# Four of eight token tiles turned by VectorE block transposes and transfers in SBUF, after the w_out product

## The chip, the cores and the metric

The kernel runs on one core of one Trainium2 chip. The metric is device time in microseconds of one execution, the median of several runs. A core has five instruction queues: TensorE (PE; its weight loads are listed as PEld), VectorE (DVE), ScalarE (ACT), GpSimd (POOL) and SyncE (SP), which here issues nearly all DMAs.

## The reference

One layer of a hybrid decoder on 1024 tokens, with 16 meta tokens ahead of them, model width 1024:

```python
z = h @ w_in + b_in                                   # q, k, v, convolution input, gates
y_attn = swa_sink_attention(q, k, v, ...) @ w_attn_proj
y_conv = silu(layer_norm(causal_dwconv(c, ...), ...)) @ w_conv_proj
mixed = sigmoid(g_attn) * y_attn + sigmoid(g_conv) * y_conv
h = layer_norm(DEEPNORM_ALPHA * h + mixed @ w_out, ln1_g, ln1_b)
up = causal_dwconv(h @ ffn_w_up, ffn_dw, ffn_dw_b)
u, g = jnp.split(up, 2, axis=-1)
f = (jax.nn.gelu(g, approximate=False) * u) @ ffn_w_down
return layer_norm(DEEPNORM_ALPHA * h + f, ln2_g, ln2_b)
```

The change sits at the line with w_out: the product, the residual, the LayerNorm, and the turn of its result into the layout that the next product, `h @ ffn_w_up`, needs.

## The kernel before

All matrix products are in float32 accuracy by splitting each operand into a high and a low part (float32r) and adding three products: high by high, high by low, low by high. ScalarE casts the high part, VectorE or GpSimd subtracts it to get the low part. `product` issues such a sum on TensorE.

The w_out product works on eight tiles of 128 tokens, with tokens on the partitions and the 1024 channels along the row. The order is 3, 7, 2, then the two last meta tokens (-1), 6, 0, 4, 1, 5. For each tile `out_rows` does two halves of 512 columns of 24 matmuls each into a PSUM bank `ps_w`; VectorE adds the residual row from `h0d` in DRAM (L1339), takes statistics (L1340), and after the second half normalizes the row (L1361). Newton's step for the reciprocal root goes through ScalarE (L268) and three small VectorE operations. The normalized row `r` lies in one of two 1024-column buffers of `RT` (part of `OB`), is stored to `h1d` in DRAM for the residual of the feed-forward part, and the buffer then takes the row load of the tile after next.

The next product needs the channels on the partitions. `turn` transposes a tile on TensorE in eight 128x128 pieces into two PSUM banks `ps_h` (L1375), and ScalarE copies them into `FA` with the LayerNorm gain and bias as scale and shift (L1385). The turn of a tile is queued on TensorE inside the tile behind it, after a half of its product, and the other half is queued after the turn. The last tile, 5, is turned inside the up projection.

The up projection is done by Strassen's scheme on 2x2 blocks, in two passes: first on `sub` 1 (the second 256 tokens of each half of the tokens: tiles 2, 3, 6, 7), then on `sub` 0 (tiles 0, 1, 4, 5). VectorE forms sums of blocks (`bsub`, L1285), and ScalarE and VectorE split them (`bsplit`, L1276 and L1281); weights are split by `wsplit` (L1405, L1406) and combined by VectorE (L1423). These steps are done between the tiles, listed in `work`, and from tile 0 on VectorE's order is written out: every operation that goes through `line` is queued behind the one before it. All other order on an engine is the scheduler's, which works with ranks (`RK_TURN` comes before `RK_SUMS`); `after` adds an order without a wait of its own. SyncE issues loads and stores in one order for all, and a DMA that has to wait holds those behind it.

Of the kernel before, what the change touches and what calls it, by code (L numbers as in the profile page):

```python
# [25 lines left out]
AF = mybir.ActivationFunctionType  # L26
# [3 lines left out]
P = 128  # L30
D = 1024
KC = D // P
# [29 lines left out]
SUB = [(0, 258), (258, HW)]  # L62


RK_TURN, RK_SPLIT, RK_EVAC, RK_START, RK_QKV, RK_RESID, RK_ATT = 450, 500, 600, 1000, 10000, 20000, 30000
# [59 lines left out]
def tile_hybrid_layer(  # L125
# [3 lines left out]
    nc = tc.nc  # L129
# [5 lines left out]
    def load(o, i):  # L135
        return nc.sync.dma_start(out=o, in_=i)
# [5 lines left out]
    def f32(ap):  # L142
        return ap.bitcast(F)

    def after(ins, first):

        tc.add_manual_dep(ins.ins, first.ins.name, mybir.DependencyInfo(
            mybir.DependencyClass.NoSync, mybir.DependencyReason.SCHED_ONLY), reason="order of work")

    @contextmanager  # L150
    def rank(p):

        saved = tc.cur_priority
        tc.cur_priority = p
        yield
        tc.cur_priority = saved
# [10 lines left out]
    RHC = arena.tile([P, 8384], R, name="RHC")  # L167
    RHO = arena.tile([P, 8384], R, name="RHO")
    OB = arena.tile([P, 4 * U], F, name="OB")
# [6 lines left out]
    h0d = dpool.tile([U, D], F, name="h0d")  # L176
    h1d = dpool.tile([S, D], F, name="h1d")
# [39 lines left out]
    cols = const.tile([P, N_COLS], F, name="cols")  # L217
# [13 lines left out]
    g1col = lambda k: colA[:, 58 + k:59 + k]  # L231
    b1col = lambda k: colA[:, 66 + k:67 + k]
# [420 lines left out]
    for k in range(8):  # L653
        scaled(2, k)
        parts(2, k, hi_act=(1, 3, 5, 7))
        if k in (3, 4, 5, 6):
# [26 lines left out]
    bias, bias0 = (bias_t[:, a:b].rearrange("p (u h c) -> p u h c", u=2, h=NH // 2)  # L683
                   for a, b in ((0, NH * KW), (NH * KW, N_BIAS)))
# [60 lines left out]
    src = ps[:16, :P].rearrange("p (g d) -> p g d", d=HD)  # L745
    nc.scalar.copy(VA[:16, 0, :, 0], src)
    nc.vector.tensor_tensor(VA[:16, 0, :, 1], src, f32(VA[:16, 0, :, 0]), OP.subtract)
    for q4 in range(2):
# [4 lines left out]
        src = ps[:, :].rearrange("p (n g d) -> p n g d", g=2, d=HD)  # L753
# [16 lines left out]
    def load_q(g, i):  # L770
        m = 0 if i else 16
        t = ap.tile([P, 8 * P + 16], R, name="qt", tag="qt", bufs=3)[:, 16 - m:]
        for h in range(2):
            load(f32(t[h * HD:(h + 1) * HD]), dram(qd, g * HD * 8 * U + q_at(i) - m, [[8 * U, HD], [1, 8 * P + m]]))
        if m:
            pairs0.append(t[:, :16].rearrange("p (l r q) -> p l r q", l=2, r=4))
        return t[:, m:].rearrange("p (u l h x) -> p l u h x", l=2, u=2, h=2)
# [7 lines left out]
    ahead = chunks_done[first_chunk + 2 * KC + 7]  # L785
# [6 lines left out]
    for h in range(NH):  # L792
        g, r = divmod(h, 4)
        o = ps[:2, h * 16:(h + 1) * 16]
# [34 lines left out]
    for g in range(NKV):  # L829
# [3 lines left out]
        src = ps[:16].rearrange("p (r q) -> p r q", r=4)[:, :, 0:2]  # L833
# [3 lines left out]
    for g in range(NKV):  # L837
        o = po[:, g * 8:g * 8 + 8]
# [21 lines left out]
    for i in range(NB):  # L860
        for g in range(NKV):
            q = load_q(g, i) if i else q0[g]
# [6 lines left out]
            for u in range(2):  # L869
# [3 lines left out]
                for h in range(2):  # L873
                    o = ps[:, h * KW:h * KW + w]
# [8 lines left out]
                if not i:  # L883
                    f = first[u]
                    src = ps[:, :2 * KW].rearrange("p (h c) -> p h c", h=2)
# [9 lines left out]
            for h in range(2):  # L895
                for u in range(2):
                    j = h * 2 + u
# [68 lines left out]
    OC = late.tile([P, 8320], R, name="OC")  # L966
# [124 lines left out]
    RT = OB[:, 0:2048]  # L1091
# [128 lines left out]
    def h1_at(sub, i):  # L1220
        return 2048 * sub + i * (SUB[sub][1] - SUB[sub][0])

    def h1F(sub, h, k):
        o = h1_at(sub, h * KC + k)
        return FA[:, o:h1_at(sub, h * KC + k + 1)]
# [28 lines left out]
    def line(ins):  # L1254

        if lined:
            after(ins, lined[-1])
        lined.append(ins)
        return ins
# [51 lines left out]

    WO_ORDER = (4, 5, 0, 1, 2, 3, 6, 7)
    edge = const.tile([P, KC, 2], F, name="edge")
    r_next = [1]

    def out_rows(i, between=(), work=()):


        n, u = (P, 2 + i * P) if i >= 0 else (2, 0)
        if n == P:  # L1320
            o = r_next[0] % 2 * 1024
            r_next[0] += 1
            whole = RT[:, o:o + 1024]
            load(whole, h0d[u:u + n, :])
        else:
            whole = OB[:, 3072:4096]
        r = whole[:n]
        order = WO_ORDER if i != 5 else (0, 1, 2, 3, 6, 7, 4, 5)
        turned = None
        st = small.tile([P, 2, 6], F, name="st")  # L1330
        pin = line if i in (0, 4, 1, 5) else lambda ins: ins
        for half in range(2):
            hs = slice(half * 512, half * 512 + 512)
            ps = pat.tile([P, 512], F, name="ps_w", tag="mm", bufs=3)
            if n == P:
                last = product(ps, [(mixed(i, k, 0), mixed(i, k, 1), wo[k][0][:, hs], wo[k][1][:, hs])
                                    for k in order], turned)
                with rank(RK_TURN):
                    pin(nc.vector.tensor_tensor(r[:, hs], ps, r[:, hs], OP.add))  # L1339
                    pin(nc.vector.bn_stats(st[:, half], r[:, hs]))  # L1340
                turned = None
                if between[half:] and between[half]:
                    turned = turn(*between[half], behind=[last])
                if half == 0:
                    for f, *x in work:
                        f(*x)
                continue

            for j in range(4):
                nc.tensor.matmul(ps[:2], sel[:, j // 2 * 2:j // 2 * 2 + 2], two_parts[j // 2][j % 2][:, hs],  # L1350
                                 start=j == 0, stop=j == 3)
            nc.scalar.copy(r[:, hs], ps[:2])
        if n < P:
            q = FA[:2, 0:1024]
            load(q, h0d[0:2, :])
            nc.vector.tensor_tensor(r, r, q, OP.add)
        with rank(RK_TURN):
            (mu, rs), = ln_stats([(r, n)], half_stats=st if n == P else None)
            for a in (512, 0) if i == 5 else (None,):
                x = r if a is None else r[:, a:a + 512]  # L1360
                ins = pin(nc.vector.tensor_scalar(x, x, mu, rs, OP.subtract, OP.mult))  # L1361
        if n == P:
            load(h1d[u - 2:u - 2 + P, :], r)
        else:
            load(ed, r)
            for t in range(2):
                load(edge[:, :, t], dram(ed, t * D, [[1, P], [P, KC]]))
        return whole, n, ins

    def turn(i, r, n, ins, banks=None, behind=None, upper=False):  # L1370
        with rank(RK_TURN):
            for j, k0 in enumerate((4, 0) if upper else (0, 4)):
                ps = banks[j] if banks else pat.tile([P, 512], F, name="ps_h", tag="s", bufs=2)
                for k in range(4):
                    ins = nc.tensor.transpose(ps[:, k * P:(k + 1) * P], r[:, (k0 + k) * P:(k0 + k + 1) * P], ident)  # L1375
                    if behind:
                        after(ins, behind[-1])
                        behind.append(ins)
                for k in range(k0, k0 + 4):
                    src = ps[:, (k - k0) * P:(k - k0 + 1) * P]  # L1380
                    h, jj = divmod(i, 4)
                    sub = 0 if jj < 2 else 1
                    a = 2 + jj * P - SUB[sub][0]
                    dst = h1F(sub, h, k)[:, a:a + P]
                    nc.scalar.activation(dst, src, AF.Identity, bias=b1col(k), scale=g1col(k))  # L1385
        return behind[-1] if behind else None


    RING = [RHO[:, i * 1024:(i + 1) * 1024] for i in range(4)]
    RING += [None] * 4  # L1390
# [81 lines left out]
    ahead = []  # L1472
# [4 lines left out]
    for i in (3, 7, 2, -1, 6, 0, 4, 1, 5):  # L1477
        if i == -1:
            out_rows(i)
            continue  # L1480
        rows = out_rows(i, ahead, work.get(i, ()))
        ahead = [None, (i, *rows)] if i == 3 else [(i, *rows)]
        if i == 3:
            two_rows(7, rows[2])
        if i == 7:
            for a, (hi, lo) in zip(two_sum, two_parts):
                after(split(a, hi, lo, True), rows[2])
            two_stack.close()
            W2.append(wo_stack.enter_context(tc.tile_pool(name="w2", bufs=1, side="right", reuse_waits="tile")).tile(
                [P, 2048], R, name="W2"))  # L1490
        if i == 0:
            form_t2(1)
        if i == 4:
            split_of(1, BT4)
            split_of(1, BT1)
            edges()
        if i == 1:
            split_of(1, BT3)
            split_of(0, B21, EARLY)
            form_t3(0, EARLY)  # L1500
            form_t4(0, EARLY)
# [64 lines left out]
    for c in range(FC):  # L1566
# [8 lines left out]
        for subs in passes:  # L1575
            last = subs == passes[-1]
            w_next = iter(range(7))
            a, b = SUB[subs[0]][0], SUB[subs[-1]][1]
            i = max(a, 2)
# [37 lines left out]
            ins = tt(c11[:, a:b], at(Z), u13[:, a:b], OP.add)  # L1617
# [23 lines left out]
            ins = tt(c22[:, i:b], c22[:, i:b], u13[:, i:b], OP.add)  # L1641
# [127 lines left out]
    rows, stats = {}, {}  # L1769
# [159 lines left out]
```

## Time and profile before

| | |
|---|---|
| median of 3 runs | 1234.69 us (1234.56 to 1234.72) |
| profiled execution | 1234.65 us |
| its span in the profile | 1232.9 us, 21777 instructions |
| TensorE, VectorE, ScalarE, GpSimd busy | 99%, 88%, 47%, 1% |
| DMA | 210.62 MB, mean 171 GB/s |
| product of w_out to start of the up projection | about 490 to 588 us from the start of the span |

A row of the timeline has the start in us from the start of the span, the duration in us, the engine, the line of the kernel, the operation, what it writes and reads, the shape and the count of merged instructions; in brackets stands how long the engine was idle before it and what ended that. SPq is the DMA issue on SyncE. Tiles of the work (3, 7, 2, ...) are not named in the rows; they follow from the order.

### The profile page before, as it was taken

The page shows a single profiled execution, that of the slowest core. Times are in us where ns is not written, and L with a number is a line of the kernel's source. Part 1 is how long each engine was busy: PE and PEld are TensorE (multiplying, and loading weights), DVE is VectorE, ACT ScalarE, POOL GpSimd, SP SyncE. Part 2 cuts the span into 40 slices and gives each one's busy share as a digit, 9 for nine tenths or more (in the row PEclk, how much of TensorE's full clock was granted, in tenths as well). Part 3 has the DMA queues.
Part 4 walks back from the last instruction along what each step waited for, and adds up shares of the span by engine and source line. Part 5 has one row for each costly group of instructions (what it writes and reads, how often), then busy time and mean ns, then how long its engine had stood idle before and what let it go on. Part 6 is the DMA issues. An engine that isn't in the chain of part 4 may idle for free.

```text
span 1232.9 us, 21777 instructions
## 1 busy us (share of the span) xinstructions
PE 1223.6 (99%) x8564; PEld 1141.3 (93%) x8564; DVE 1084.5 (88%) x1840; ACT 584.4 (47%) x1065; POOL 15.0 (1%) x19
## 2 busy tenths in 40 slices
PE   9999999999999999999999999999999999999997
PEld 8999999999999999888999999999999998888886
DVE  8899989999879798659899999998999986995697
ACT  7532346654265233435655545555455553544331
POOL 1000000000000010000000000000000000000000
PEclk9999999999999999999999999999999999999999
DMA  7284834412255544322255555554465568997722
GB/s 280 74 277 101 213 96 112 129 55 73 85 153 175 180 140 136 116 73 87 69 182 197 193 191 197 191 187 137 167 210 190 182 230 305 395 334 295 255 87 86
DMA packets 104726, 210.62 MB, mean 171 GB/s; under 512 B 28520, under 2 KB 42394, under 8 KB 104624
## 3 DMA queue, kind: packets, MB, share of 16 engines
q1 hardware_dynamic: 88624, 198.16, 48.6%
q10 hardware_dynamic: 16000, 11.07, 2.9%
q8 instruction: 67, 1.10, 0.4%
q14 instruction: 35, 0.29, 0.1%
HBM read 147.59 MB, written 60.38 MB: 169 GB/s over the span
## 4 chain that ended last, share of the span: by engine, by line
PE 98%; DVE 1%; ACT 0%; issue 0%; DMA 0%; POOL 0%; DVEq 0%; POOLq 0%
PE px L1596 14%; PE py L1596 9%; PE ps_x L1742 9%; PE ps_z L330 8%; PE ps_z L329 8%; PE ps_z L325 8%; PE ps_z L1742 8%; PE pw L1596 5%; PE pz L1596 5%; PE ps_p L325 2%; PE ps_p L329 2%; PE ps_p L330 2%; PE ps_w L329 2%; PE ps_w L330 2%; PE ps_w L325 2%; PE ps_z L565 2%
## 5 line engine op out<-in xcount | busy, mean ns | idle before, releaser
L715 DVE SCALAR_TENSOR_TENSOR FA<-cin,cols,FA 128x1026 f32<-128x1026 f32 x120 | 152.3, 1278 | 0.9
L330 PE MATMUL ps_z<-RHO,wlo 128*128 128x256 f32 (+2 forms) x324 | 103.6, 320 | 0.0
L329 PE MATMUL ps_z<-RHO,whi 128*128 128x256 f32 (+2 forms) x324 | 103.5, 319 | 0.0
L330 PE MATMUL ps_z<-RHC,wlo 128*128 128x256 f32 (+2 forms) x324 | 103.4, 319 | 0.0
L329 PE MATMUL ps_z<-RHC,whi 128*128 128x256 f32 (+2 forms) x324 | 103.4, 319 | 0.0
L325 PE MATMUL ps_z<-RHC,whi 128*128 128x256 f32 (+2 forms) x324 | 103.2, 319 | 0.0
L325 PE MATMUL ps_z<-RHO,whi 128*128 128x256 f32 (+2 forms) x324 | 103.2, 318 | 0.0
L294 ACT CAST whi<-wr 128x1024 fp32r<-128x1024 f32 x37 | 38.9, 1051 | 107.4 <-PE ps_z L329 85.1
L1405 ACT CAST RHO<-wr 128x512 fp32r<-128x512 f32 x92 | 55.3, 619 | 26.2 <-DMA wr<-in_w_up_dram 12.2
L1406 DVE TENSOR_TENSOR RHO<-wr,RHO 128x512 fp32r<-128x512 f32 x92 | 62.4, 690 | 5.2 <-ACT RHO L1405 4.9
L325 PEld LDWEIGHTS ps_z<-RHO,whi 128*128 128x128 f32 x324 | 60.9, 188 | 4.5
L329 PEld LDWEIGHTS ps_z<-RHO,whi 128*128 128x128 f32 x324 | 60.9, 188 | 4.2
L325 PEld LDWEIGHTS ps_z<-RHC,whi 128*128 128x128 f32 x324 | 60.9, 188 | 4.1
L329 PEld LDWEIGHTS ps_z<-RHC,whi 128*128 128x128 f32 x324 | 61.0, 188 | 4.1
L330 PEld LDWEIGHTS ps_z<-RHO,wlo 128*128 128x128 f32 x324 | 61.0, 188 | 4.0
L330 PEld LDWEIGHTS ps_z<-RHC,wlo 128*128 128x128 f32 x324 | 61.0, 188 | 3.9
L1423 DVE TENSOR_TENSOR wr<-wr 128x512 f32<-128x512 f32 x88 | 60.9, 692 | 0.2
L297 DVE TENSOR_TENSOR wlo<-wr,whi 128x1024 fp32r<-128x1024 f32 x35 | 42.7, 1221 | 12.0 <-ACT whi L294 11.6
L1608 ACT COPY FA<-px 128x514 f32<-128x514 f32 (+2 forms) x23 | 13.1, 569 | 71.1 <-PE px L1596 71.0
L1405 ACT CAST ws<-wr 128x512 fp32r<-128x512 f32 x60 | 36.1, 618 | 20.9 <-DVE wr L1423 11.8
L722 ACT ACTIVATE FA<-ps_z,cols 128x258 f32<-128x258 f32 (+2 forms) x48 | 26.1, 543 | 39.4 <-PE ps_z L330 39.0
L1406 DVE TENSOR_TENSOR ws<-wr,ws 128x512 fp32r<-128x512 f32 x60 | 40.6, 688 | 3.6 <-ACT ws L1405 3.5
(487 smaller groups left out, 3492.2 us busy)
## 6 DMA issues: line engine op xcount, KB each, us to landing
wr<-in_w_up_dram SPq DMA_DIRECT2D x44, 512.0 KB
wr<-in_w_z_dram SPq DMA_DIRECT2D x30, 512.0 KB
fd<-FA SPq DMA_DIRECT2D x44, 256.0 KB
OB<-in_w_down_dram SPq DMA_DIRECT2D x19, 512.0 KB
qt<-qd SPq DMA_DIRECT2D x28, 256.0 KB
td<-OB SPq DMA_DIRECT2D x12, 512.0 KB
sums<-fd SPq DMA_DIRECT2D x12, 512.0 KB
sd<-sums SPq DMA_DIRECT2D x12, 512.0 KB
```

Of the source, the lines that this page charges most:

```text
L294: ins = nc.scalar.copy(hi, raw)
L297: return (nc.vector if quick else nc.gpsimd).tensor_tensor(lo, raw, f32(hi), OP.subtract)
L325: ins = nc.tensor.matmul(ps, ah, bh, start=i == 0, stop=False)
L329: nc.tensor.matmul(ps, ah, bl, start=False, stop=False)
L330: last = nc.tensor.matmul(ps, al, bh, start=False, stop=i == n - 1)
L715: nc.vector.scalar_tensor_tensor(acc[c], cin[:, j:j + U], wc, acc[c], OP.mult, OP.add)
L722: nc.scalar.activation(t, ps, AF.Tanh, bias=bcol(14 + i), scale=0.5)
L1405: nc.scalar.copy(hi, src)
L1406: ins = nc.vector.tensor_tensor(lo, src, f32(hi), OP.subtract)
L1423: ins = nc.vector.tensor_tensor(*x)
L1596: ins = nc.tensor.matmul(o, x[:, ks], bmat(sub, q, hl, k), start=first and k + j == 0, stop=k == 3 and j == 2, skip_group_check=not first)
L1742: nc.tensor.matmul(bank[:, cs], l[:, ts], r[:, ws], start=first and a and x + k == 0, stop=z and x == len(ops) - 1 and k == 2, skip_group_ ...
```

## The change

Tiles 3, 7, 2 and 0 are no longer turned on TensorE. After the normalization VectorE does one `transpose` over 128x1024, which turns every 32x32 block in its place and sorts the blocks by the partition group they go to; 16 transfers in SBUF (32 partitions of 1 KB each) bring the blocks to their partitions, into a free stretch of `OC` or `RHC`; and eight ScalarE copies read them from there into `FA` with the same scale and shift as before. For tile 0 the transpose has a place in VectorE's written order, right after the normalization. Tiles 6, 4, 1 and 5 are turned as before.

The row loads, the stores of normalized rows and the transfers get one written order on SyncE (`in_turn`): the load of the tile after next comes after the tile's transfers, or, for tiles turned on TensorE, after the turn. Before, these were in the scheduler's order.

```diff
+    NROW = (3, 7, 2, 6, 0, 4, 1, 5)
+    NEXT_ROWS = dict(zip(NROW, NROW[2:]))
+    moves, fetched = [], {}
+
+    def in_turn(ins):
+        if moves:
+            after(ins, moves[-1])
+        moves.append(ins)
+
+    def fetch(i):
+        o = (NROW.index(i) + 1) % 2 * 1024
+        fetched[i] = RT[:, o:o + 1024]
+        in_turn(load(fetched[i], h0d[2 + i * P:2 + (i + 1) * P, :]))
...
         if n == P:
-            o = r_next[0] % 2 * 1024
-            r_next[0] += 1
-            whole = RT[:, o:o + 1024]
-            load(whole, h0d[u:u + n, :])
+            if i not in fetched:
+                fetch(i)
+            if not moves[1:]:
+                fetch(NROW[1])
+            whole = fetched[i]
...
                     turned = turn(*between[half], behind=[last])
+                    if between[half][0] in NEXT_ROWS:
+                        fetch(NEXT_ROWS[between[half][0]])
...
-            load(h1d[u - 2:u - 2 + P, :], r)
+            in_turn(load(h1d[u - 2:u - 2 + P, :], r))
...
+    TURN_AT = {3: (OC, 4144, 2048), 7: (OC, 5168, 2048), 2: (OC, 6192, 2048), 0: (RHC, 2096, 3072)}
+
+    def turn_dma(i, r, norm):
+        t, o, b = TURN_AT[i]
+        blocks, cols = OB[:, b:b + 1024], f32(t[:, o:o + 1024])
+        with rank(RK_TURN):
+            ins = nc.vector.transpose(blocks.rearrange("p (q k j) -> p q k j", q=4, k=KC),
+                                      r.rearrange("p (k q j) -> p q k j", k=KC, q=4))
+            after(ins, norm)
+            if i in (0, 4):
+                line(ins)
+            for a in range(4):
+                for q in range(4):
+                    in_turn(load(cols[32 * q:32 * q + 32, a * 256:(a + 1) * 256],
+                                 blocks[32 * a:32 * a + 32, q * 256:(q + 1) * 256]))
+            if i in NEXT_ROWS:
+                fetch(NEXT_ROWS[i])
+            h, jj = divmod(i, 4)
+            sub = 0 if jj < 2 else 1
+            a = 2 + jj * P - SUB[sub][0]
+            src = cols.rearrange("p (a k j) -> p k a j", a=4, k=KC)
+            for k in range(KC):
+                nc.scalar.activation(h1F(sub, h, k)[:, a:a + P].rearrange("p (a j) -> p a j", a=4), src[:, k],
+                                     AF.Identity, bias=b1col(k), scale=g1col(k))
...
         rows = out_rows(i, ahead, work.get(i, ()))
-        ahead = [None, (i, *rows)] if i == 3 else [(i, *rows)]
+        ahead = [] if i in TURN_AT else [(i, *rows)]
+        if i in TURN_AT:
+            turn_dma(i, rows[0], rows[2])
```

More of the change, by code (lines that the diff above doesn't have):

```diff
@@ L1313, in tile_hybrid_layer @@
     edge = const.tile([P, KC, 2], F, name="edge")
-    r_next = [1]
+    NROW = (3, 7, 2, 6, 0, 4, 1, 5)
[9 more added lines that the diff above has]
+        in_turn(load(fetched[i], h0d[2 + i * P:2 + (i + 1) * P, :]))
     def out_rows(i, between=(), work=()):
```

## The prediction

> **What bounds the kernel now.** I read the page first (busy shares, clock, chain), then the stretch of the w_out product in windows, then the chain of waits there in order of time, then the timelines of VectorE, TensorE's weight loads, ScalarE and SyncE's DMA issues.
>
> ```profile
> span 1232.9 us, 21777 instructions
> PE 1223.6 (99%) x8564; PEld 1141.3 (93%) x8564; DVE 1084.5 (88%) x1840; ACT 584.4 (47%) x1065; POOL 15.0 (1%) x19
> PEclk9999999999999999999999999999999999999999
> PE 98%; DVE 1%; ACT 0%; issue 0%; DMA 0%; POOL 0%; DVEq 0%; POOLq 0%
> ```
>
> TensorE is busy for 99% of the span, at full clock, and holds 98% of the chain. So whatever is taken out of TensorE's own queue is worth its full length, as long as no other engine then becomes late. The profiled execution took 1234.65 us, 1.75 more than its span and 0.04 below the median of 1234.69; all sums below are against 1234.65.
>
> ```profile
> 530.00:540.00 10.00, 10.00 (x50) 8.36 (x49) 5.65 (x14) 5.07 (x11) 0.00 (x0) 1.00 0.25 80
> 550.00:560.00 10.00, 10.00 (x49) 8.36 (x49) 9.07 (x14) 4.06 (x9) 0.00 (x0) 1.00 0.16 57
> 560.00:570.00 10.00, 10.00 (x48) 8.29 (x47) 9.11 (x15) 5.14 (x10) 0.00 (x0) 1.00 0.15 56
> 570.00:580.00 10.00, 10.00 (x49) 8.34 (x48) 9.25 (x19) 5.30 (x12) 0.00 (x0) 1.00 0.27 100
> ```
>
> The columns after the window are PE, PEld, DVE, ACT, POOL, clock, DMA share and GB/s. The product of the eight token tiles runs from about 490 to 588 us. TensorE never pauses there. VectorE is half idle until about 546 (5.65 of 10 us), and over 90% busy from 550 on, when tiles 0, 4 and 1 are summed and normalized between the forming and splitting of the next matrix product's operands. The first half of the stretch has room on VectorE, the second has hardly any; tiles 3, 7 and 2 lie in the first, tile 0 at the start of the second.
>
> **Part 1, what leaves TensorE.** The chain shows the turns of tiles 3, 7, 2 and 0, each eight transposes of 128x128:
>
> ```profile
> 515.71 0.87 PE ps_h L1375 x8
> 520.69 0.87 PE ps_h L1375 x8
> 534.37 0.87 PE ps_h L1375 x8
> 557.93 0.87 PE ps_h L1375 x8
> ```
>
> All four are on the chain, and nothing fills the place where they stood, so TensorE is earlier by 3 x 0.87 = 2.61 us from 535 on and by 4 x 0.87 = 3.48 us from 559 on. That is the whole gain there can be: 1234.65 - 3.48 = 1231.17. The turns of 6, 4, 1 and 5 stay.
>
> **Part 2, what VectorE gets: one block transpose of 128x1024 float32 per tile.** There is no such instruction in the trace. These rows bound it, and show the queue it is put into (start, duration, line; in brackets the idle time before it):
>
> ```profile
> 532.40 0.81 DVE L1361 TENSOR_SCALAR OB<-OB,mv,sd 128x1024 f32<-128x1024 f32 x1
> 540.73 0.69 DVE L1339 TENSOR_TENSOR OB<-ps_w,OB 128x512 f32<-128x512 f32 x1 [4.91 <-PE ps_w L330]
> 543.34 0.81 DVE L1361 TENSOR_SCALAR OB<-OB,mv,sd 128x1024 f32<-128x1024 f32 x1
> 546.18 0.69 DVE L1339 TENSOR_TENSOR OB<-ps_w,OB 128x512 f32<-128x512 f32 x1 [2.03 <-PE ps_w L330]
> 552.53 0.69 DVE L1339 TENSOR_TENSOR OB<-ps_w,OB 128x512 f32<-128x512 f32 x1 [0.32 <-PE ps_w L330]
> 555.14 0.81 DVE L1361 TENSOR_SCALAR OB<-OB,mv,sd 128x1024 f32<-128x1024 f32 x1
> 555.87 1.22 DVE L1285 TENSOR_TENSOR FA<-FA 128x1024 f32<-128x1024 f32 x1
> 557.12 1.23 DVE L1285 TENSOR_TENSOR OB<-FA 128x1024 f32<-128x1024 f32 x1
> 558.26 0.68 DVE L1339 TENSOR_TENSOR OB<-ps_w,OB 128x512 f32<-128x512 f32 x1
> 562.43 1.22 DVE L1281 TENSOR_TENSOR OC<-OB,OC 128x1024 fp32r<-128x1024 f32 x1
> 563.83 0.69 DVE L1406 TENSOR_TENSOR RHO<-wr,RHO 128x512 fp32r<-128x512 f32 x1 [0.18 <-ACT RHO L1405]
> 568.18 0.81 DVE L1361 TENSOR_SCALAR OB<-OB,mv,sd 128x1024 f32<-128x1024 f32 x1
> 568.91 1.22 DVE L1281 TENSOR_TENSOR RHC<-FA,RHC 128x1024 fp32r<-128x1024 f32 x1
> 579.43 0.81 DVE L1361 TENSOR_SCALAR OB<-OB,mv,sd 128x1024 f32<-128x1024 f32 x1
> 585.04 0.69 DVE L1406 TENSOR_TENSOR RHO<-wr,RHO 128x512 fp32r<-128x512 f32 x1
> 587.87 0.69 DVE L1339 TENSOR_TENSOR OB<-ps_w,OB 128x512 f32<-128x512 f32 x1 [2.14 <-PE ps_w L330]
> ```
>
> A pass over 128x1024 takes VectorE's queue 0.73 us at its fastest (568.18 to 568.91) and 1.14 at its ordinary pace (557.12 to 558.26). I take 1.14, the row with the same shape and type that isn't on the fast form; 0.73 is the lower end, two passes, 2.28, the upper. Below nothing it cannot be: the instruction is new work.
>
> For tiles 3, 7 and 2 it costs nothing: the 4.91 us of idle time at 540.73 cover it (the place of tile 2's), and the tiles before have as little on VectorE. If that cover were gone it would cost 1.14 each.
>
> For tile 0 it lands where VectorE has no room. It is pinned between tile 0's normalization (555.14) and the first sum of operands (555.87), and all that follows in the written order moves by 1.14. Who waits for it? Tile 4's normalization (568.18, done at 568.99) is in that order, and TensorE's turn of tile 4 reads it:
>
> ```profile
> 545.75 1.03 PEld L1375 LDWEIGHTS ps_h<-cols,OB 128*128 128x128 f32 x8
> 569.32 1.03 PEld L1375 LDWEIGHTS ps_h<-cols,OB 128*128 128x128 f32 x8
> 581.11 1.02 PEld L1375 LDWEIGHTS ps_h<-cols,OB 128*128 128x128 f32 x8
> ```
>
> Before, TensorE came to it at 569.32, with 0.33 us in hand. After, TensorE comes at 569.32 - 3.48 = 565.84. VectorE starts its dense run with tile 0's second half, which TensorE brings 2.61 us earlier (552.53 becomes 549.92). From there to 568.99 it has no room but two waits of 0.36 us on ScalarE for a reciprocal root and the 0.18 at 563.83. That last one I take to vanish, since ScalarE no longer has the eight evictions of tile 0 there. So tile 4 is normalized at 568.99 - 2.61 + 1.14 - 0.18 = 567.34, and TensorE stands still for 567.34 - 565.84 = 1.50 us with tile 1's second half queued behind the turn. The net gain falls to 3.48 - 1.50 = 1.98.
>
> Is it lost or gained again later? Tile 1 is normalized at 580.24 - 1.65 = 578.59, and TensorE comes to its turn at 581.11 - 1.98 = 579.13: no second wait. At 587.87 VectorE had been idle for 2.14 us after ending at 585.73; 1.81 of them remain (584.08 against 585.89), so its delay ends there, and the up projection starts 1.98 us earlier than before.
>
> **Part 3, SyncE and the transfers.** Each tile adds 16 transfers of 32 KB (32 partitions of 1 KB) in SBUF. Nothing in the trace is quite like them. Issue rows:
>
> ```profile
> 555.98 0.32 SPq L136 DMA_DIRECT2D h1d<-OB  x1
> 558.84 0.32 SPq L136 DMA_DIRECT2D OB<-h0d  x1
> 3.08 1.48 SPq L136 DMA_DIRECT2D x<-in_x_dram  x3
> ```
>
> An issue takes 0.32 us alone and 1.48 / 3 = 0.49 in a crowd. A store takes 2.86 us from issue until the row load that waits for it (558.84 - 555.98). I take 0.32 and 2.86. For tile 0 the transpose ends at 555.95 - 2.61 + 1.14 = 554.48, the last transfer is issued at 554.48 + 15 x 0.32 = 559.28 and lands at 562.14. Its first user is the early operand split (573.42 below, 1.98 earlier: 571.44), 9.3 us later, less 2.90 for the eight ScalarE copies. So the transfers themselves are hidden. The row load for tile 1 is queued behind the 16 issues; it goes at 559.6 and is there by 562.5, while TensorE doesn't end tile 1's first half before 567.3 (569.32 less 1.98). Tile 2 is normalized at 533.21 - 1.74 and turned by 532.6 (two turns are gone by then); its transfers are issued until 537.7, and the row load behind them lands at 540.9, against 546.18 - 2.61 = 543.57: 2.7 us in hand. At 0.49 each nothing is left of that. The transfers of tile 3 and 7 meet no deadline nearer than this.
>
> The Trainium skill, DMA: Bandwidth & Descriptors, section Bandwidth, says to batch transfers to 1 MiB and calls those under 64 KB descriptor-dominated. It speaks against 64 transfers of 32 KB, and the sum by it is that of rival two, 1236.2, where the rows give 1232.7. No row of this trace shows such small ones one behind another.
>
> **Part 4, ScalarE.** Eight scale-and-shift copies per tile from SBUF take the place of eight from PSUM; the count is the same and I cost the work at nothing.
>
> ```profile
> 542.43 0.29 ACT L268 ACTIVATE sd<-mv,eps 128x1 f32<-128x1 f32 x1 [2.81 <-DVE mv L261]
> 558.41 2.90 ACT L1385 ACTIVATE FA<-ps_h,cols 128x128 f32<-128x128 f32 x8 [0.24 <-PE ps_h L1375]
> 561.16 1.09 ACT L1276 CAST OC<-OB 128x1024 fp32r<-128x1024 f32 x1
> 562.10 1.70 ACT L1405 CAST RHO<-wr 128x512 fp32r<-128x512 f32 x3
> 573.42 0.67 ACT L1276 CAST RHC<-FA 128x520 fp32r<-128x520 f32 x1
> ```
>
> What is new is the wait: the copies now wait for transfers, and ScalarE runs in order. That is the rival below.
>
> The sum: 1234.65 - 3.48 + 1.50 = 1232.67, so 1232.7. With the ends of the transpose (0.73 and 2.28) it is 1232.3 and 1233.8.
>
> **Rival one, the whole gain.** VectorE's run proves looser than I read it (the transpose close to the fast pass and the waits on ScalarE swallowed), and TensorE doesn't wait for tile 4: 1231.2. For it: the run had 0.33 us in hand and three small waits. Against it: they sum to 1.2 us, and 0.87 + 1.14 is asked for.
>
> **Rival two, ScalarE held by the transfers, slower than before.** If tile 0's copies stand in ScalarE's queue where they stood (558.41), they hold it until the last transfer lands, 562.14, and then for 2.90, to 565.04. Behind them wait the cast at 561.16 and the weight casts at 562.10, and VectorE's pinned order waits for those. If only the weight casts are behind, VectorE's step of 563.83 (562.18 after) starts at 565.04 + 0.62 instead: 3.5 us of further delay, all of it paid at the turn of tile 4, and the time is 1232.7 + 3.5 = 1236.2. If the cast of 561.16 is behind too, the step of 562.43 (560.96 after) starts at 566.1: 5.2 us, 1237.9. At 0.49 an issue 2.6 more are paid: 1238.8 and 1240.5. Slower by more than 0.2% begins with only the weight casts behind at 0.39 us an issue. Against it: the order of ScalarE may well put the copies later, since nobody needs them before 571.
>
> The Trainium skill, VectorE: DVE Perf Modes, section Rules for kernel authors, says to transpose 128x128 on TensorE where a PSUM destination will do, as it does here; by that rule the change gives back more than it saves, and the mechanism here would be that of this rival.
>
> **Rival three, the same one tile earlier.** Tile 2's copies could hold the reciprocal root of tile 6 (542.43, 539.82 after): transfers landing at 540.3 (537.4 + 2.86), copies until 543.2, the root 3.4 us late, against 1.6 us in hand at TensorE's turn of tile 6 (normalized at 544.15, read at 545.75). That costs about 1.8 us before the dense run begins, and it moves both engines alike: 1234.5.
>
> **How the numbers follow.** 0.2% is 2.5 us (about what a measurement here can tell from no change): faster is below 1232.2, slower above 1237.2. My forecast has 0.40, own range 1231.9 to 1233.8, a quarter of it below 1232.2. Rival one has 0.18, faster. Rival two has 0.30, half of it slower. Rival three has 0.07, same. Transfers that go nearly one after another have 0.05, slower: 0.9 us from one landing to the next would bring tile 0 to its first user too late. That makes faster 0.28, same 0.52, slower 0.20. The range from 1231.1 to 1237.9 leaves out most of the slower half of rival two and the last case, and little below.
>
> **What would show it.** Right: no turns of 3, 7, 2 and 0 on TensorE; a transpose of about 1.2 us after each of their normalizations; TensorE idle for 1.5 us ahead of tile 4's turn with VectorE's L1361 as the releaser, and nowhere else before 588; the same steps 2 us earlier from there on. Wrong: a wait of ScalarE on DMA between 556 and 566, a wait at tile 6's turn, or transposes far from 1.14.

## The result, and the profile after

The kernel after takes 1246.77 us (1245.84 to 1247.29), the kernel before beside it 1234.62: a ratio of 1.0098, 95% interval 1.0083 to 1.0112. It is 12.1 us slower. The forecast was 1232.7, and the range ended at 1237.9. The profiled execution took 1246.54 us, 11.89 more than the one of before.

From the page of after, the span, the busy shares, the granted clock and the chain by engine:

```profile
span 1244.7 us, 21836 instructions
PE 1222.3 (98%) x8532; PEld 1139.2 (92%) x8532; DVE 1088.1 (87%) x1844; ACT 586.7 (47%) x1065; POOL 15.0 (1%) x19
PEclk9999999999999999998999999999999999999999
PE 93%; SPq 2%; DVE 2%; DMA 2%; issue 0%; ACT 0%; POOL 0%; DVEq 0%; ACTq 0%; POOLq 0%
```

TensorE has 32 instructions fewer, which are the four turns, and is busy for less time; the span is longer all the same. The chain now holds 2% of SyncE's issue (SPq), 2% of VectorE and 2% of transfers; before it held 98% of TensorE and next to nothing else. Windows over the w_out product (columns as in the prediction: PE, PEld, DVE, ACT, POOL, clock, DMA share, GB/s):

```profile
520.00:530.00 10.00, 7.25 (x32) 4.58 (x30) 2.14 (x4) 4.89 (x12) 0.00 (x0) 1.00 0.47 141
540.00:550.00 10.00, 8.79 (x44) 7.11 (x43) 5.23 (x10) 4.92 (x14) 0.00 (x0) 1.00 0.50 143
570.00:580.00 10.00, 1.13 (x6) 0.70 (x5) 8.46 (x15) 5.53 (x12) 0.00 (x0) 0.66 0.30 89
```

TensorE stands still for 2.75 us in the first, 1.21 in the second and 8.87 in the third. In the timeline of TensorE the waits have their places:

```profile
526.88 1.09 PE L1365 MATMUL ps_w<-OC,sel 128*2 128x512 f32 x4 [0.72 <-ACT OB L1367]
530.05 0.50 PE L325 MATMUL ps_w<-RX,RHC 128*128 128x512 f32 x1 [2.08 <-DVE OB L1352]
547.87 1.09 PE L1390 MATMUL ps_h<-cols,OB 128*128 128x128 f32 x8 [1.21 <-DVE OB L1376]
579.62 1.94 PE L1390 MATMUL ps_h<-cols,OB 128*128 128x128 f32 x8 [8.87 <-DVE OB L1376]
581.79 0.63 PE L329 MATMUL ps_w<-RX,RHO 128*128 128x512 f32 x1
583.44 0.39 PE L330 MATMUL ps_w<-RW,RHO 128*128 128x512 f32 x1
```

TensorE waits there for ScalarE's copy of the meta tokens' product (L1367), for the residual sum of tile 2 (L1352), for the normalization of tile 6 and, longest, for that of tile 4 (L1376). VectorE waits in turn for rows and for transfers:

```profile
526.45 1.25 DVE L1410 STREAM_TRANSPOSE OB<-OB 128x1024 f32<-128x1024 f32 x1 [6.25 <-DMA OC<-OB]
529.30 1.29 DVE L1352 TENSOR_TENSOR OB<-ps_w,OB 128x512 f32<-128x512 f32 x2 [1.60 <-DMA OB<-h0d]
540.26 1.25 DVE L1410 STREAM_TRANSPOSE OB<-OB 128x1024 f32<-128x1024 f32 x1 [3.50 <-DMA OC<-OB]
555.27 0.69 DVE L1352 TENSOR_TENSOR OB<-ps_w,OB 128x512 f32<-128x512 f32 x1 [7.46 <-DMA OB<-h0d]
578.66 0.81 DVE L1376 TENSOR_SCALAR OB<-OB,mv,sd 128x1024 f32<-128x1024 f32 x1
599.74 0.69 DVE L1352 TENSOR_TENSOR OB<-ps_w,OB 128x512 f32<-128x512 f32 x1 [2.89 <-PE ps_w L330]
```

And the rows are late because SyncE is still issuing transfers. Its timeline (start, length of the run of issues, count):

```profile
514.70 10.09 SPq L136 DMA_DIRECT2D OC<-OB  x16
524.83 0.58 SPq L136 DMA_DIRECT2D OB<-h0d  x1
525.53 0.35 SPq L136 DMA_DIRECT2D h1d<-OB  x1
527.73 10.97 SPq L136 DMA_DIRECT2D OC<-OB  x16
538.74 0.58 SPq L136 DMA_DIRECT2D OB<-h0d  x1
539.91 0.24 SPq L136 DMA_DIRECT2D ed<-OB  x1
541.53 10.02 SPq L136 DMA_DIRECT2D OC<-OB  x16
551.60 0.60 SPq L136 DMA_DIRECT2D OB<-h0d  x1
565.93 10.02 SPq L136 DMA_DIRECT2D RHC<-OB  x16
```

Sixteen issues hold SyncE for 10.0 to 11.0 us, 0.63 each, where the prediction had 5.1. The rows of tiles 2, 6 and 0 (the loads at 524.83, 538.74 and 551.60) leave right behind them, and there each takes 0.58 to 0.60 us itself. A second wait comes with it: tiles 3, 7 and 2 put their turned blocks into the same columns of `OB`, so the transposes of 7 and 2 wait until the transfers of the tile before have been read out (6.25 and 3.50 us).

The largest wait can be followed to its end. The row load of tile 0 was to land at 540.9. Tile 2's transfers start at 541.53 instead of 532.6, 8.9 us late. SyncE stood still for 1.85 us ahead of tile 7's transfers (525.88 to 527.73) and for 1.38 us ahead of tile 2's (540.15 to 541.53), each time until the transpose was done; so the shared columns account for about 3.2 of the 8.9 us, and the rest goes back to the issue. No run gives the tiles columns of their own, so this split is worked out and not shown. The issue of tile 2's transfers takes 4.9 us more than the 5.1 allowed; the load lands when VectorE goes on, about 555.2. VectorE takes tile 0's first half at 555.27, where before it was at 546.18, 9.1 us later. From there on its queue is dense, so tile 4 is normalized at 579.47 instead of 568.99: the 9.1, 1.2 for tile 0's transpose and 0.2 (tile 4's root comes 0.8 us late behind the first of tile 0's copies, and small waits of before are gone). TensorE, only 1.0 us later than before at that point (its last matmul ahead of the turn starts at 570.36, before at 569.31), stands still for 8.87.

The sum up to the same step of both kernels, tile 5's first residual sum at 587.87 before and 599.74 after, is +11.87, all of the 11.89. The turns give -3.48 and the idle time 0.72 + 2.08 + 1.21 + 8.87 = +12.88. After a pause the next matmul also comes 0.16 later than the idle time tells, since matmuls of 0.39 follow each other every 0.23: four pauses, +0.64. The remaining 1.8 is the clock after the long pause: the turn holds the queue for 1.60 instead of 0.87 (581.22 - 579.62), and the matmuls behind it take 0.63 instead of 0.39 until 583.44.

### The profile page after: what moved, and what is told of

Read it like the earlier page. It is cut to its first block, busy times and chain, and to the rows that moved or that the text cites. A ratio compares the mean times of both kernels' runs of the same rounds, so it can differ in the third digit from the quotient of the medians.

```text
span 1244.7 us, 21836 instructions
## 1 busy us (share of the span) xinstructions
PE 1222.3 (98%) x8532; PEld 1139.2 (92%) x8532; DVE 1088.1 (87%) x1844; ACT 586.7 (47%) x1065; POOL 15.0 (1%) x19
## 4 chain that ended last, share of the span: by engine, by line
PE 93%; SPq 2%; DVE 2%; DMA 2%; issue 0%; ACT 0%; POOL 0%; DVEq 0%; ACTq 0%; POOLq 0%
PE px L1638 14%; PE py L1638 10%; PE ps_x L1784 9%; PE ps_z L330 8%; PE ps_z L329 8%; PE ps_z L325 8%; PE ps_z L1784 8%; PE pz L1638 5%; PE pw L1638 5%; PE ps_p L325 2%; PE ps_p L329 2%; PE ps_p L330 2%; SPq L136 2%; PE ps_z L565 2%; PE ps_o L925 1%; PE ps_s L876 1%
## 5 line engine op out<-in xcount | busy, mean ns | idle before, releaser
L1638 PE MATMUL px<-OA,RHO 128*128 128x258 f32 (+1 forms) x336 | 43.6, 279 | 0.0
```

The costliest lines, as they stand in the source:

```text
L1638: ins = nc.tensor.matmul(o, x[:, ks], bmat(sub, q, hl, k), start=first and k + j == 0, stop=k == 3 and j == 2, skip_group_check=not first)
```

## The experiments

Theory: the time is lost because an issue of an SBUF-to-SBUF transfer holds SyncE for 0.6 us, so that row loads queued behind 16 of them are late. Rivals: the written order; the transposes on VectorE; ScalarE, held by copies that wait for transfers (the prediction's rivals two and three); the transfers as such, wherever they are queued.

**The written order alone.** All eight tiles on TensorE, as before:

```diff
+    TURN_AT = {}
...
-        ahead = [] if i in TURN_AT else [(i, *rows)]
+        ahead = [] if i in TURN_AT else [None, (i, *rows)] if i == 3 else [(i, *rows)]
```

> All eight tiles are turned on TensorE as before the change; only the written order of stores and row loads on SyncE is kept. The theory (16 transfers in SBUF at about 0.63 us of issue each hold SyncE for 10 us per tile, and the row loads queued behind them come late) expects no cost of the order itself: 1234.6 us, within 1. The rival that the written order alone holds the row loads back expects a good part of the 12 us: over 1238.

1234.75 us, ratio 1.0001 (0.9991 to 1.0010). The order of stores and loads by itself costs nothing that shows.

**No transfers.**

```diff
-            for a in range(4):
-                for q in range(4):
-                    in_turn(load(cols[32 * q:32 * q + 32, a * 256:(a + 1) * 256],
-                                 blocks[32 * a:32 * a + 32, q * 256:(q + 1) * 256]))
...
-            src = cols.rearrange("p (a k j) -> p k a j", a=4, k=KC)
+            src = blocks.rearrange("p (a k j) -> p k a j", a=4, k=KC)
```

> Leaves out the 64 transfers: VectorE's block transposes stay, ScalarE's copies read the blocks where they lie (so part of the rearrangement is left out). The theory expects the time that the prediction gave for VectorE's part alone, 1232.7 us (1231.5 to 1234), with TensorE waiting 1 to 2 us ahead of tile 4's turn. The rival that VectorE's transposes in its written order carry the loss expects over 1240.

1232.78 us, ratio 0.9984 (0.9975 to 0.9994): the prediction's number. The timelines of VectorE and TensorE at tile 0's transpose and tile 4's turn:

```profile
553.30 1.25 DVE L1410 STREAM_TRANSPOSE OB<-OB 128x1024 f32<-128x1024 f32 x1
554.46 1.18 DVE L1285 TENSOR_TENSOR FA<-FA 128x1024 f32<-128x1024 f32 x1
566.47 0.81 DVE L1376 TENSOR_SCALAR OB<-OB,mv,sd 128x1024 f32<-128x1024 f32 x1
567.43 1.06 PE L1390 MATMUL ps_h<-cols,OB 128*128 128x128 f32 x8 [1.31 <-DVE OB L1376]
```

The transpose holds VectorE's queue for 1.16 us (554.46 - 553.30; predicted 1.14), tile 4 is normalized at 567.28 (predicted 567.34), and TensorE waits 1.31 there (predicted 1.50). The whole loss of 14 us hangs on the transfers and on what waits for them, and VectorE's part is as predicted.

**Three tiles instead of four**, tile 0 back on TensorE:

```diff
+    TURN_AT = {i: TURN_AT[i] for i in (3, 7, 2,)}
```

> The change for tiles 3, 7 and 2 only, 48 transfers in SBUF on SyncE, tile 0 turned on TensorE. Theory: the late row loads come from tiles 7 and 2, so most of the loss stays, less the transpose and the copies in the dense part: 1241 to 1245 us. The rival that tile 0's transfers and copies carry the loss expects 1233 or less.

1244.37 us, ratio 1.0076 (1.0062 to 1.0090). The row of tile 0 is as late as in the change (VectorE waits 6.89 us for it); tile 0's own transfers are the small part of what costs.

**The transfers on GpSimd's queue**, so that SyncE has only rows and stores:

```diff
-                    in_turn(load(cols[32 * q:32 * q + 32, a * 256:(a + 1) * 256],
-                                 blocks[32 * a:32 * a + 32, q * 256:(q + 1) * 256]))
+                    nc.gpsimd.dma_start(out=cols[32 * q:32 * q + 32, a * 256:(a + 1) * 256],
+                                        in_=blocks[32 * a:32 * a + 32, q * 256:(q + 1) * 256])
```

> The same 64 transfers, issued by GpSimd instead of SyncE; stores and row loads keep their order on SyncE. The theory expects the row loads on time again and 1232 to 1236 us, unless GpSimd issues so slowly that tile 2's data come late for the operand sums. The rival that the transfers' own time (VectorE's next transpose waits until the shared block buffer has been read) carries the loss expects 1240 or more, with the waits of VectorE on the transfers still there.

1341.90 us, ratio 1.0868 (1.0850 to 1.0886). A miss, and it doesn't separate the theories, for GpSimd is slower still. Two neighbours from its timeline:

```profile
519.70 0.51 POOL L1417 DMA_DIRECT2D OC<-OB  x1 [3.73 <-issue]
521.73 0.51 POOL L1417 DMA_DIRECT2D OC<-OB  x1 [1.51 <-issue]
```

One leaves every 2.0 us, some 34 us for a tile's 16, and all operands behind them come late.

**Fewer, larger transfers: one store to DRAM and four loads per tile.**

```diff
+    bd = dpool.tile([4, P, D], F, name="bd")
...
-            for a in range(4):
-                for q in range(4):
-                    in_turn(load(cols[32 * q:32 * q + 32, a * 256:(a + 1) * 256],
-                                 blocks[32 * a:32 * a + 32, q * 256:(q + 1) * 256]))
+            n = list(TURN_AT).index(i)
+            in_turn(load(bd[n], blocks))
+            for q in range(4):
+                in_turn(load(cols[32 * q:32 * q + 32].rearrange("p (a c) -> p a c", a=4),
+                             dram(bd, n * P * D + q * 256, [[D, 32], [32 * D, 4], [1, 256]])))
```

> Per tile one store of the blocks to DRAM and four loads of 32 partitions from there, instead of 16 transfers in SBUF, all on SyncE in the same place of the order. The theory expects five issues of 0.32 us and one wait of about 3 us for the store, so SyncE is held for about 5 us instead of 10, row loads 5 us earlier, and 1233 to 1237 us. The rival that the path length (transfers landing late for ScalarE) carries the loss expects no gain over the change, since the way by DRAM is longer: 1244 or more.

1247.22 us, ratio 1.0101 (1.0086 to 1.0116). A miss that taught something. From the timelines of SyncE, ScalarE and TensorE:

```profile
518.69 1.76 SPq L136 DMA_DIRECT2D OC<-bd  x4
544.43 3.18 ACT L1428 ACTIVATE FA<-OC,cols 128x128 f32<-128x128 f32 x8 [8.43 <-DMA OC<-bd]
549.77 1.97 PE L1390 MATMUL ps_h<-cols,OB 128*128 128x128 f32 x8 [5.28 <-DVE OB L1376]
579.62 1.94 PE L1390 MATMUL ps_h<-cols,OB 128*128 128x128 f32 x8 [4.99 <-DVE OB L1376]
```

SyncE issues for 2.1 us a tile only (0.32 and 1.76), though it also stands still ahead of the loads, 2.3 to 6.4 us a tile, at the least until the store has landed. But now ScalarE stands still for 8.43 us with tile 2's copies at the head of its queue and the root of tile 6 behind them, and TensorE waits at the turns of tiles 6 and 4: the prediction's rivals three and two. So there are two causes. In the kernel by DRAM the copies alone cost about 12 us: with them later it is 1235.73, as shown below.

**The copies later**, queued on ScalarE behind the next tile's normalization; transfers as in the change:

```diff
+            copies(pending.pop(), rows[2])
...
-                nc.scalar.activation(h1F(sub, h, k)[:, a:a + P].rearrange("p (a j) -> p a j", a=4), src[:, k],
-                                     AF.Identity, bias=b1col(k), scale=g1col(k))
+                ins = nc.scalar.activation(h1F(sub, h, k)[:, a:a + P].rearrange("p (a j) -> p a j", a=4), src[:, k],
+                                           AF.Identity, bias=b1col(k), scale=g1col(k))
+                after(ins, norm)
```

> The change with its 64 transfers in SBUF, but ScalarE's copies of a turned tile are queued behind the normalization of the tile after it. If the row loads held back by the 10 us of issue carry the loss (theory), this gains only the 0.8 us of ScalarE's root that waited behind tile 0's copies: 1244 to 1247 us, VectorE still waiting about 7 us for tile 0's row. If ScalarE held by the copies carries it (rival), 1235 or less.

1246.93 us, ratio 1.0098 (1.0084 to 1.0112), the change's own ratio. VectorE still waits 7.25 us for the row of tile 0. In the change the rows bind and the copies don't.

**Half of the transfers.** This puts SyncE at about the time that the prediction had allowed:

```diff
-                for q in range(4):
+                for q in range(2):
```

> Leaves out half of the rearrangement: 8 of a tile's 16 transfers. 8 issues at 0.60 us hold SyncE for 4.8 us a tile, about the 5.1 us (16 at 0.32) that the prediction took for the 16. Theory (the issue price is the one mis-sized term): the rows are there in time, TensorE waits 1.3 to 1.5 us at tile 4's turn alone, and the prediction's own number comes out, 1232.4 to 1233.2. Rival (ScalarE, held by copies that wait for the transfers, costs time at the predicted issue price too): the root of tile 6 or the operand casts behind tile 0's copies come late, 1234.5 to 1238.

1238.23 us (1237.49 to 1239.95), ratio 1.0030 (1.0018 to 1.0041). The rival's side of the expectation, 0.2 above its range. From the timelines of SyncE, ScalarE, VectorE and TensorE:

```profile
532.90 6.04 SPq L136 DMA_DIRECT2D OC<-OB  x8
540.34 2.81 ACT L1426 ACTIVATE FA<-OC,cols 128x128 f32<-128x128 f32 x7 [7.69 <-DMA OC<-OB]
543.37 0.16 DVE L276 SCALAR_TENSOR_TENSOR sd<-mv,sd 128x1 f32<-128x1 f32 x1 [3.50 <-ACT sd L268]
544.82 1.09 PE L1390 MATMUL ps_h<-cols,OB 128*128 128x128 f32 x8 [1.21 <-DVE OB L1376]
562.53 3.19 ACT L1426 ACTIVATE FA<-RHC,cols 128x128 f32<-128x128 f32 x8
566.26 0.69 DVE L1446 TENSOR_TENSOR RHO<-wr,RHO 128x512 fp32r<-128x512 f32 x1 [2.47 <-ACT RHO L1445]
571.56 1.38 PE L1390 MATMUL ps_h<-cols,OB 128*128 128x128 f32 x8 [3.86 <-DVE OB L1376]
```

No row is late enough to stop TensorE any more. What stops it are tile 2's copies ahead of tile 6's root (VectorE waits 3.50 us for it, of which 0.36 is usual; rival three had it 3.4 late) and tile 0's copies ahead of a weight cast (rival two). The sum of both rivals' prices on the forecast, 1232.7 + 1.8 + 3.5 = 1238.0, is near the median, but that is chance. TensorE waits 1.21 us at tile 6's turn where rival three had 1.8, and 3.86 at tile 4's where 1.50 of the forecast and 3.5 of rival two make 5.0; both prices were too high. Behind the 3.86 us the clock drops, which no price held, and tile 2's eight transfers held SyncE for 6.04 us, 0.9 more than the 5.1 allowed. The profiled execution is also the longest of the six (1239.95).

**Half of the transfers, and the copies later.** That the 5.5 us are ScalarE's is only argued so far; this run moves the copies alone.

> Half of the transfers left out as in the run with 8 of 16 (1238.2), and the copies queued on ScalarE behind the next tile's normalization. Theory (at the issue time that the prediction took, ScalarE's hold is what stands between its 1232.7 and 1238.2: 1.2 us at tile 6's turn, 3.9 at tile 4's): both holds go, tile 4's VectorE wait of 1.3 to 1.5 us stays, 1232.7 to 1234.2. Rival (the transfers or their issues cost the 5.5 us in another way): above 1236.5.

1234.00 us (1233.3 to 1236.6), ratio 0.9998 (0.9989 to 1.0007). Both holds are gone, and 4.2 of the 5.5 us with them. What remains in the waits of TensorE on VectorE's normalizations is tile 4's (us in all, times, the longest):

```profile
PE ps_h L1390 <- DVE OB L1376: 2.0, 1, 2.0
```

That is 0.5 us more than the forecast's 1.50; where the rest of the 1.3 us goes stays open.

**The row load ahead of the 16 transfers, and the copies later**; all 64 transfers in SBUF:

```diff
+            if i in NEXT_ROWS:
+                fetch(NEXT_ROWS[i])
             for a in range(4):
                 for q in range(4):
                     in_turn(load(cols[32 * q:32 * q + 32, a * 256:(a + 1) * 256],
                                  blocks[32 * a:32 * a + 32, q * 256:(q + 1) * 256]))
-            if i in NEXT_ROWS:
-                fetch(NEXT_ROWS[i])
```

> The change with its 64 transfers in SBUF, the row load queued ahead of the 16 transfers of its tile and the copies behind the next tile's normalization. Theory (a row load's place behind 16 issues on SyncE is what costs): the rows of tiles 2, 6 and 0 are no longer late by over 2 us, most of the 12 us goes, 1233.5 to 1238, what stays being stores and copies that come late behind the transfers. Rival (the transfers themselves slow VectorE or TensorE, wherever they are queued): above 1243.

1247.72 us, ratio 1.0107 (1.0093 to 1.0121). A miss: the theory had said that most of the 12 us would go. The timelines of SyncE, ScalarE and VectorE:

```profile
515.04 10.30 SPq L136 DMA_DIRECT2D OC<-OB  x16
528.75 11.17 SPq L136 DMA_DIRECT2D OC<-OB  x16
543.31 10.02 SPq L136 DMA_DIRECT2D OC<-OB  x16
554.70 3.19 ACT L1431 ACTIVATE FA<-OC,cols 128x128 f32<-128x128 f32 x8 [5.94 <-DMA OC<-OB]
558.85 2.36 DVE L1281 TENSOR_TENSOR OC<-FA,OC 128x1024 fp32r<-128x1024 f32 x2 [9.66 <-ACT OC L1276]
```

The row loads are no longer behind the 16 of their own tile, but the stores are. The next row load waits until such a store has landed, the next tile's transfers stand behind that load, and its transpose still waits until the shared columns have been read out. Tile 2's transfers are issued until 553.3, its copies come at 554.70, and the operand splits that need them keep VectorE waiting for 9.66 us. So my theory was too narrow: not the place of the row loads, but the 31 us that three tiles' issues take of SyncE, with nearly 7 us of stores, row loads and waits between them, is what costs: between the end of tile 3's transpose (515) and the splits (about 549) lie only 34. With the order turned round, what comes late is the data instead of the rows. The row of tile 0 is late by 4.0 us still. The rival's number came out as well, above 1243; but the splits themselves run at their usual 1.2 us each (2.36 for two), and what VectorE waits for is the data, so nothing here shows an engine slowed by the transfers.

**By DRAM with the copies later** (both edits above together), so without either cause, on four tiles and on three:

> The way by DRAM (one store, four loads per tile) with the copies queued behind the normalization of the next tile. In the run by DRAM the row loads were on time and ScalarE's copies, waiting for the data, held the reciprocal roots and weight casts behind them (VectorE idle 7.1 and 3.6 us for ScalarE). Theory of two holds, one on SyncE and one on ScalarE: with both gone only the transpose in VectorE's order is left, 1232.7 us as without transfers, 1232 to 1234.5. The rival that the data themselves come too late for the operand sums expects over 1238.

> As the run by DRAM with later copies, but tile 0 turned on TensorE as before the change; only 3, 7 and 2 go around. Theory: the three turns of 0.87 us are gained and nothing is put into VectorE's dense order, so TensorE does not wait for tile 4: 1234.65 - 2.61 = 1232.0 (1231.5 to 1233). If the transpose in the dense order cost nothing, this would be slower than with four tiles by 0.9 us.

1235.73 us, ratio 1.0012 (1.0003 to 1.0021), with four, and 1234.46, ratio 0.9997 (0.9988 to 1.0006), with three. Eleven of the 12 us are back, but both lie above the range that was expected, by 1.2 and 1.5 us: the row of tile 2 is still late by some tenths, and the splits of the operands of tiles 2 and 3 stand behind tile 2's copies (VectorE waits 1.4 and 1.2 us for them). With four, TensorE then waits 2.75 us at tile 4's turn.

**By DRAM, row load ahead of the four loads, copies later**, on three tiles and on two (the first expectation is that for three; its "run before" is the one with two):

```diff
+    TURN_AT = {i: TURN_AT[i] for i in (3, 7,)}
...
             in_turn(load(bd[n], blocks))
+            if i in NEXT_ROWS:
+                fetch(NEXT_ROWS[i])
             for q in range(4):
```

> As the run before with tile 2 too. Theory: the row of tile 2 in time gives back 0.6 to 0.9 us of the three-tile run with the row load behind the loads (1234.46), the casts behind tile 2's copies still cost 0.4 to 0.8: 1233.3 to 1234.0. Rival (the late casts behind tile 2's copies are the larger part): 1234.2 or more, no better than with two tiles.

> Tiles 3 and 7 alone, by one store to DRAM and four loads, row load ahead of the four loads, copies behind the next tile's normalization; tiles 2 and 0 stay on TensorE. Theory (two turns are worth 2 x 0.87 once no row is late and no cast stands behind tile 2's copies): 1234.7 - 1.7 = 1233.0, from 1232.8 to 1233.5. Rival (the transposes on VectorE or the written order cost what the turns give): 1234.3 to 1235.0.

With three, 1234.51 us, ratio 0.9998 (0.9989 to 1.0007), no better than with the row load behind; there the rival was right, the casts behind tile 2's copies are the larger part. With two, **1232.90 us** (1232.65 to 1233.33), ratio 0.9985 (0.9977 to 0.9994), as expected: 1.8 us for two turns of 0.87. It beats before and after, before by little. The windows of two tiles, then of three:

```profile
540.00:550.00 10.00, 10.00 (x50) 8.36 (x49) 7.43 (x13) 4.77 (x11) 0.00 (x0) 1.00 0.30 105
560.00:570.00 10.00, 10.00 (x50) 8.36 (x49) 9.24 (x18) 4.47 (x10) 0.00 (x0) 1.00 0.14 54
```
```profile
550.00:560.00 10.00, 9.46 (x47) 7.69 (x46) 9.15 (x14) 4.93 (x12) 0.00 (x0) 1.00 0.18 63
560.00:570.00 10.00, 9.15 (x45) 7.45 (x44) 9.29 (x16) 4.49 (x8) 0.00 (x0) 1.00 0.18 71
```

With two, TensorE does not stop from 500 to 590; with three, it loses 1.39 us again, over half of its 2.61.

## Why the prediction was wrong

**Part 1, the turns: right.** Four turns of 0.87 leave TensorE, and two of them, where nothing else is late, are worth 1.8.

**Part 2, VectorE: right.** 1.14 was taken for the transpose, 1.16 measured; the wait at tile 4's turn was 1.31 for 1.50 as long as no transfer was in the way. The forecast's number comes out once the transfers are left out. The rule that was weighed here, to transpose 128x128 on TensorE (the Trainium skill, VectorE: DVE Perf Modes, section Rules for kernel authors), is borne out here for four tiles (1246.77, and 1235.73 by DRAM, against 1234.7) and, by a little, not for two: 1232.90 against 1234.71.

**Part 3, SyncE: the step that failed.** "I take 0.32 and 2.86" was the wrong row, and the term that it gives, 16 issues in 5.1 us, measured 10.0 us. 0.32 is the issue of a store or load between SBUF and DRAM. The price of an issue between two places in SBUF stood in the trace of before, in the view of the tile `va` (durations in ns, least, median, most):

```profile
L136 SPq DMA_DIRECT2D va<-v x2: 642/667/692, 85.9 to 86.6; - x2
```

These two move 448 and 512 KB and so are not the same transfer, but their median of 0.67 us is near the 0.59 of the new ones (0.63 with the gaps between). The prediction had even worked out where it tips: 2.7 us in hand behind tile 2's transfers, and "at 0.49 each nothing is left of that". At 0.63 the 16 take 10.0 us, 4.9 more than 5.1, and the hand is overdrawn in one tile already. Two further sentences failed with it. "The transfers of tile 3 and 7 meet no deadline nearer than this" overlooked that a tile's delay is handed to the next, by SyncE's one order and by the place that the three tiles share for their blocks (8.9 us by tile 2, about 3.2 of them by the shared place). And "the transfers themselves are hidden" was worked out for tile 0 alone: with the row loads ahead of the transfers, the data of tile 2 came late instead (1247.72).

Beside it stands the rule that the prediction weighed: the Trainium skill, DMA: Bandwidth & Descriptors, section Bandwidth, against transfers under 64 KB. The trace agrees with its direction: SyncE issues for 10.0 us for 512 KB in 16 pieces and for 2.1 in five. The sum that I had given by it, 1236.2, was far too low.

**Part 4, ScalarE: the work at nothing was nearly right, the order wrong.** Eight copies take 3.19 us from SBUF and 2.90 from PSUM. But "the order of ScalarE may well put the copies later" is refuted by the run with half the transfers: the scheduler puts them at the head, and there they hold it. So the forecast would have failed at about the issue price that it assumed too, only with some 1238 instead of 1247. Rivals two and three were not alternatives to be given 0.30 and 0.07, but came together there; of their prices, 3.5 and 1.8, the run shows 2.4 (3.86 less the 1.50 of the forecast) and 1.21. In the change itself the late rows hide most of both; what shows is the 0.8 us of tile 4's root.

**The range and the signs.** The change is slower by more than 0.2%, which had 0.20. The nearest case, transfers that go nearly one after another, had 0.05 and was asked at which landing interval tile 0 would be late; it is the issue, not the landing, that goes one after another, and tile 2 that is late. Of the marks named for wrong, the wait at tile 6's turn was seen (1.21), but in the change it came from tile 6's late row. The wait of ScalarE between 556 and 566 was not seen, and the transposes took their 1.16.

**A term that was missing: the clock.** All sums were made at full clock. After the 8.87 us pause the windows of after, of 2 us each, show:

```profile
572.00:574.00 2.00, 0.00 (x0) 0.00 (x0) 2.00 (x3) 0.98 (x2) 0.00 (x0) 0.78 0.20 49
574.00:576.00 2.00, 0.00 (x0) 0.00 (x0) 1.97 (x4) 0.65 (x1) 0.00 (x0) 0.50 0.21 52
582.00:584.00 2.00, 2.00 (x7) 1.59 (x7) 1.97 (x4) 2.00 (x7) 0.00 (x0) 0.66 0.04 10
```

TensorE stops at 570.75, the granted clock falls to 0.50 some 2.4 us later and is full again about 3.7 us after the restart; this costs 1.8 us. The length of a pause alone does not tell whether the clock falls. The pause of 2.08 us at 530 did not lower it (1.00 in its window), and one of 2.75 us at tile 4's turn by DRAM with the copies later did not either; one of 2.12 us, for tile 2's row with three tiles, did (the clock was 0.50 from 530 to 532, and the matmul behind the pause took 0.79 us instead of the 0.50 shown above at 530.05), and so did the 3.86 us with half the transfers.

```profile
530.08 0.79 PE L325 MATMUL ps_w<-RX,RHC 128*128 128x512 f32 x1 [2.12 <-DVE OB L1352]
```

The Trainium skill, TensorE: Matmul & The Clock Gate, Part 1, gives about 3.4 us of idle time for the fall and of work for the rise, in a window that is free-running. The runs agree in the rise (3.7); the fall came sooner, 2.4 us after TensorE stopped here and within a pause of 2.12 us there.

## What to carry to other kernels

Price a DMA issue by its route and count: take the row that moves data between the same two memories, multiply by the number of issues, and hold the product against the time until the next row load or store of that queue is due. An operation on an in-order engine that waits for a transfer costs what is queued behind it; if nobody needs it soon, queue it behind the next urgent step. Move as many tiles as the cover holds, not as many as can be moved: here, by DRAM, two were worth 1.8 us, three nothing, four a loss of 1.0.

## What the runs showed of the hardware

- An issue on SyncE takes 0.59 us (0.63 with its gap) between two places in SBUF, 32 partitions of 1 KB; 0.32 for a store of 128 rows of 4 KB to DRAM or a load from there, but 0.58 to 0.60 for such a load right behind the 16; 0.44 for a load of 32 partitions of 4 KB from DRAM in four pieces each (1.76 for four).
- GpSimd sends out one such SBUF transfer every 2.0 us.
